# Turning the rotated queries and keys and the differential heads' outputs on VectorE and by block transfers, with score tiles of their own, in a two-layer encoder trunk

## The chip, the cores and the metric

The kernel runs on one core of a Trainium2 chip. The metric is the device time of one execution in microseconds (us), the median of several. One profiled execution is read instruction by instruction. The engines go by the names of the profile: PE (TensorE, matrix products), PEld (its weight loads), DVE (VectorE), ACT (ScalarE), POOL (GpSimd), SP (SyncE, which here only issues DMAs). A name with a q at its end (SPq) is the engine's instruction queue. Each engine works its queue off in order.

## The reference, cut to what matters

Two layers run over 256 tokens of width 2048, all in fp32. Layer 0 mixes with dilated window attention (8 heads) beside differential attention (4 heads); layer 1 mixes with grouped-query attention (8 query heads on 2 key heads, normalised and rotated) beside neighbourhood attention (8 heads). A gated convolutional FFN follows each mixer.

```python
# differential attention (layer 0): two softmax maps, then a norm over each head's 256 outputs
p = jax.nn.softmax(logits, axis=-1)
w = p[:, :, 0] - lam * p[:, :, 1]
o_b = jnp.einsum("bhqk,bkhd->bqhd", w, vf)
o_b = rmsnorm(o_b, subln) * (1.0 - lambda_init)
# grouped-query attention (layer 1)
q_c = apply_rope(rmsnorm(q_c, q_norm), cos, sin)
k_c = apply_rope(rmsnorm(k_c, k_norm), cos, sin)
o_c = gqa_block_attention(q_c, k_c, v_c)
# both layers
mixed = jnp.concatenate([out_1, out_2], axis=-1)
h = h + jnp.einsum("bse,ed->bsd", mixed, w_out)
h = h + conv_ffn(rmsnorm(h, ln_ffn), ...)
```

## The kernel before

**Products.** Each fp32 operand is split into a high part (rounded to fp32r, by ACT) and a rest (by DVE), and a product is three products of such parts: high by high, high by rest, rest by high. The helper is `split` (L239; `split_scaled`, L245, scales as well), so most casts and subtractions stand under L240 and L243.

**Weights** come in units of 512 KB, 128 partitions by 1024 numbers. `wunit` (L116) issues one DMA on SP (L125) into one of five `raw` tiles and splits it into one of four `wh` and four `wl` tiles. `gemm_a` (L208, products L204 to L206) makes a 256x512 chunk from eight or eleven units, twelve products each. `gemm_b` (L151, products L142 and L148) makes two 128x256 feature tiles from four units: high products of all units first, then the rests. Products accumulate in PSUM: four banks "gm" for the gemms, two "s" for scores and head outputs, two "tp" for what PE transposes.

**Order.** One clock of ticks lays the small work between the large. `tick` advances after every two units of `gemm_a` and twice in a `gemm_b`, so a tick is about two units. `later(d, f, rank)` (L91) puts off `f` by d ticks, `flush` (L103) ticks until nothing is pending. The functions only write instructions down in this order; the framework then sets the order of each engine's queue by its own reckoning of what is ready, keeping dependencies, so an instruction can stand ahead of one written earlier.

**Turning.** A 128x128 block is turned in one of two ways. `transpose_block` (L302) uses PE, by products with the identity (L305), into a "tp" bank. `turned` (L286) lets DVE transpose each 32x32 square in place (L288) and then `moved` (L278) carries the squares to their places by sixteen DMAs (L282), of which SP and POOL issue eight each, row by row in turn.

**Differential heads.** For each of the four heads, `gemm_b` makes q and k for both maps, `b_logits` and `b_softmax` follow two ticks later, `b_softmax` turns the weights (`turned`), three ticks later `b_transposes` splits them, one tick later `b_values` (L748) multiplies by the values: twelve products (L755 to L757), squares and a square root on ACT, and the scaled rows `o` (tile `ob`, L765). One tick later `b_finish` (L768) transposes `o` by PE, four blocks, and splits it into the head's two `mix` tiles, which the output projection reads. The values' order of tokens is by parity; `parity_rev` puts it straight.

**Output projection.** `mixer_out` (L369) makes four chunks of eight units; unit u reads `mix` tiles 2u and 2u+1. It runs units 0 to 6 of chunks 0 and 1 (four "gm" banks), then flushes, then runs unit 7 of both and chunks 2 and 3. Tiles 14 and 15, unit 7's, are the last head's.

**Grouped-query heads.** `norm_rope` (L838) normalises and rotates; its results are the row tiles `ry`. Three ticks later `to_features` (L872) transposes them by PE and splits them into the `cq` tiles: two key heads in one call, four query heads in each of two calls. The heads of a group follow at one a tick: `c_head` (L902) makes scores (`logits`, L426 to L428), takes the exponent on ACT (L910) into a tile `scc`, of which there are two for all heads, and `finish_head` (L888) turns it into a place in `room` (heads 0, 1, 4, 5) or in a pair tile (2, 3, 6, 7). Three ticks later the turned weights are split (tile `pt`), and a tick later `head_out` (L462, products L467 to L469) makes the head's output. The neighbourhood heads (`d_head`, L917) share `finish_head` and `scc`; one comes every two ticks.

Of the kernel before, what the change touches and what calls it, by code (L numbers as in the profile page):

```python
# [68 lines left out]
def trunk_kernel(ctx: ExitStack, tc, a, out):  # L69
# [155 lines left out]

    def parity(ap):

        return bass.AP(tensor=ap.tensor, offset=ap.offset, ap=[list(ap.ap[0]), [1, P], [P, 2]])
# [140 lines left out]
    def mixer_out(src, act, gain):  # L369
# [3 lines left out]
        for c in range(2):  # L373
            for u in range(7):
                a_unit(pss[c], src[c], u, act, KT)
                if u % 2 == 1:
                    tick()
        flush()
        for c in range(2):
            a_unit(pss[c], src[c], 7, act, KT)  # L380
            finish_chunk(pss[c], c, gain, res, 1 + c)
# [366 lines left out]
    def b_values(hd, pt, vt):  # L748
# [17 lines left out]
        later(1, lambda: b_finish(hd, o), 0)  # L766

    def b_finish(hd, o):  # L768
        ps = two(tps("tp", 2))
        transpose_block([(ps[:, f, t * P:(t + 1) * P], o[:, t, f * P:(f + 1) * P])  # L770
                         for f in range(2) for t in range(2)])
        for f in range(2):
            y = new_act("mix", 8 + 2 * hd + f)
            split_scaled(natural(y[:, 0, :]), natural(y[:, 1, :]), parity_rev(ps[:, f, :]), sub_gain[:, f:f + 1])
            mix[8 + 2 * hd + f] = y
# [96 lines left out]
    def to_features(ys, nh, slot):  # L872
        res = []
        ps = [two(tps("tp", 2)) for _ in range(nh // 2)]
        transpose_block([(ps[i // 2][:, i % 2, t * P:(t + 1) * P], ys[t][:, i, :])
                         for i in range(nh) for t in range(2)])
        for i in range(nh):
            q = new_qk("cq", slot + i)
            split(q[:, 0, :], q[:, 1, :], ps[i // 2][:, i % 2, :])
            res.append(q)  # L880
        return res
# [6 lines left out]
    def finish_head(sc, vt, cs, order, slot):  # L888
        if slot >= 8 or slot % 4 < 2:
            pf = room[:, slot % 2 * 4:slot % 2 * 4 + 4]  # L890
        else:
            if slot % 4 == 2:
                pairs[0] = pair_tile(22)
            pf = pairs[0][:, slot % 2 * 4:slot % 2 * 4 + 4]
# [5 lines left out]
        later(3, probs, 1)  # L900

    def c_head(q, k, vt, cs, slot):  # L902
# [5 lines left out]
        sc = tmp.tile([P, 2, SEQ], F32, name=nm("scc"), tag="scc")  # L908
# [26 lines left out]
    later(3, lambda ys=ys: kc.extend(to_features(ys, 2, 4)))  # L935
    for n in range(2):
# [3 lines left out]
        def c_heads(n=n, ys=ys):  # L940
            for i, q in enumerate(to_features(ys, 4, 0)):
                later(1 + i, lambda i=i, q=q: c_head(q, kc[n], cv, slice(n * P, (n + 1) * P), 4 * n + i))
        later(3, c_heads)
# [218 lines left out]
```

## Time and profile before

| | us |
|---|---|
| timed runs, median of 3 | 2466.28 (2465.97 to 2466.30) |
| the profiled execution, its own time | 2461.37 |
| its span, first to last instruction | 2459.6 |
| VectorE busy | 1636.1 |
| ScalarE busy | 1261.4 |
| products of the gemms' high parts, L142 | 956.8 |
| all transposes by PE of `ob` and `ry`, L305, 36 | 5.7 |

A row of a timeline gives start, duration, engine, line, operation, tiles written and read, and in brackets the idle time of the engine before it with what ended it. The durations of products overlap, since products are pipelined; the distance from start to start is what one costs. A row of the waits gives who waited for whom, the total, the number and the longest. A row of the windows gives the stretch, its length, and for PE, PEld, DVE, ACT and POOL the busy time with the number of instructions.

### The profile page before, as it was taken

To read this page: it belongs to the slowest core of one execution; us is meant where nothing else is said; L and a number is where in the kernel's file an instruction comes from. 1 tells how busy PE (TensorE), PEld (TensorE's weight loads), DVE (VectorE), ACT (ScalarE), POOL (GpSimd) and SP (SyncE) were. 2 spreads that over 40 slices of the span, in tenths; PEclk is the share of its full clock that TensorE was granted. 3 is DMA by queue.
4 is the path that set the end of the run, shared out by engine and by line. 5 is a ranking of instruction groups with operands and counts; after the bars stand their busy time and mean duration, and the time that the engine had idled before them with its cause. 6 is when DMAs were issued, how large, how long until landed. Compare 5 with 4: busy or idle time off the path is not lost.

```text
span 2459.6 us, 35236 instructions
## 1 busy us (share of the span) xinstructions
PE 2441.2 (99%) x12926; PEld 2108.2 (86%) x12926; DVE 1636.1 (67%) x2480; ACT 1261.4 (51%) x1876; POOL 198.3 (8%) x356
## 2 busy tenths in 40 slices
PE   9999999999999999999999999999999999999998
PEld 8888888888788888888888887888888888888887
DVE  6577577676676774477775568776767654676754
ACT  6555455565655443454544466555554533545443
POOL 1011012011200000000001106432000000000000
PEclk9999999999999999999999999999999999999999
DMA  8566566556655556565566655757555565555564
GB/s 310 184 200 191 172 195 210 174 181 198 199 184 194 186 198 196 180 198 183 195 197 207 209 175 152 224 176 224 192 184 196 181 206 196 180 192 186 193 201 146
DMA packets 194477, 476.12 MB, mean 194 GB/s; under 512 B 75384, under 2 KB 78200, under 8 KB 194304
## 3 DMA queue, kind: packets, MB, share of 16 engines
q1 hardware_dynamic: 182480, 461.09, 57.3%
q0 software_dynamic: 11392, 12.13, 2.8%
q8 instruction: 101, 1.65, 0.3%
q14 instruction: 72, 0.59, 0.1%
q10 hardware_dynamic: 432, 0.66, 0.1%
HBM read 458.48 MB, written 2.18 MB: 187 GB/s over the span
## 4 chain that ended last, share of the span: by engine, by line
PE 94%; DMA 2%; DVE 1%; ACT 1%; issue 1%; SPq 1%; POOL 0%; DVEq 0%; POOLq 0%; ACTq 0%
PE gm L142 36%; PE gm L148 19%; PE gm L205 12%; PE gm L204 12%; PE gm L206 12%; SPq L282 1%; DMA pair<-scc 0%; ACT wh L240 0%; DVE wl L243 0%; DMA room<-scc 0%; DMA hT<-z 0%; PE tp L305 0%; DMA raw<-in_od_out 0%; DMA raw<-in_od_qk 0%; PE s L428 0%
## 5 line engine op out<-in xcount | busy, mean ns | idle before, releaser
L243 DVE TENSOR_TENSOR wl<-raw,wh 128x1024 fp32r<-128x1024 f32 (+1 forms) x860 | 1034.5, 1216 | 563.0 <-ACT wh L240 328.1
L240 ACT CAST wh<-raw 128x1024 fp32r<-128x1024 f32 (+1 forms) x860 | 897.1, 1047 | 713.6 <-PE gm L206 375.8
L142 PE MATMUL gm<-yT,wh 128*128 128x512 f32 x4096 | 956.8, 390 | 3.5 <-ACT wh L240 3.0
L142 PEld LDWEIGHTS gm<-yT,wh 128*128 128x128 f32 x4096 | 760.3, 188 | 159.2 <-ACT wh L240 4.9
L148 PEld LDWEIGHTS gm<-yT,wl 128*128 128x128 f32 x4096 | 507.7, 192 | 9.3
L148 PE MATMUL gm<-yT,wl 128*128 128x256 f32 x4096 | 511.8, 283 | 0.0
L204 PE MATMUL gm<-wh,prod 128*128 128x512 f32 x702 | 273.2, 389 | 0.0
L205 PE MATMUL gm<-wl,prod 128*128 128x512 f32 x702 | 273.2, 389 | 0.0
L206 PE MATMUL gm<-wh,prod 128*128 128x512 f32 x702 | 273.1, 389 | 0.0
L233 ACT COPY t<-gm 128x256 f32<-128x256 f32 x256 | 95.2, 372 | 276.9 <-PE gm L148 276.9
L204 PE MATMUL gm<-wh,yT 128*128 128x512 f32 x412 | 161.6, 394 | 0.0
L205 PE MATMUL gm<-wl,yT 128*128 128x512 f32 x412 | 161.5, 392 | 0.0
L206 PE MATMUL gm<-wh,yT 128*128 128x512 f32 x412 | 161.3, 392 | 0.0
L204 PEld LDWEIGHTS gm<-wh,prod 128*128 128x128 f32 x702 | 131.8, 188 | 27.4
L206 PEld LDWEIGHTS gm<-wh,prod 128*128 128x128 f32 x702 | 131.8, 188 | 27.3
L205 PEld LDWEIGHTS gm<-wl,prod 128*128 128x128 f32 x702 | 131.8, 188 | 27.1
L234 DVE TENSOR_TENSOR t<-t,gm 128x256 f32<-128x256 f32 x256 | 105.5, 412 | 1.0 <-ACT t L233 0.8
L282 POOL DMA_DIRECT2D hT<-z x72 | 41.4, 583 | 785.0 <-ACT junk L274 681.0
L204 PE MATMUL gm<-wh,mix 128*128 128x512 f32 x256 | 99.9, 390 | 0.6 <-ACT mix L246 0.6
L205 PE MATMUL gm<-wl,mix 128*128 128x512 f32 x256 | 99.9, 390 | 0.4 <-DVE wl L243 0.4
L206 PE MATMUL gm<-wh,mix 128*128 128x512 f32 x256 | 99.3, 389 | 0.0
L206 PEld LDWEIGHTS gm<-wh,yT 128*128 128x128 f32 x412 | 77.8, 189 | 16.3
(247 smaller groups left out, 1669.3 us busy)
## 6 DMA issues: line engine op xcount, KB each, us to landing
raw<-in_up SPq DMA_DIRECT2D x352, 512.0 KB, 4.3
raw<-in_down SPq DMA_DIRECT2D x176, 512.0 KB, 4.2
raw<-in_eva_qk SPq DMA_DIRECT2D x96, 512.0 KB, 4.3
raw<-in_eva_v SPq DMA_DIRECT2D x46, 512.0 KB, 4.4
raw<-in_evb_qk SPq DMA_DIRECT2D x32, 512.0 KB, 4.2
raw<-in_ev_out SPq DMA_DIRECT2D x32, 512.0 KB, 4.3
raw<-in_od_qk SPq DMA_DIRECT2D x32, 512.0 KB, 4.8
raw<-in_od_out SPq DMA_DIRECT2D x32, 512.0 KB, 4.6
```

The source lines that it names most:

```text
L142: T.matmul(ps.rearrange("p a b -> p (a b)"), wh[:, k * P:(k + 1) * P], act[u * 8 + k].rearrange("p a b -> p (a b)"), start=(u == 0 and k = ...
L148: T.matmul(ps[:, 1, :], wl[:, k * P:(k + 1) * P], act[u * 8 + k][:, 0, :], start=False, stop=(last and u * 8 + k == KT - 1))
L204: T.matmul(ps[t], ah, wh[:, sl], start=(kt == 0), stop=False)
L205: T.matmul(ps[t], ah, wl[:, sl], start=False, stop=False)
L206: T.matmul(ps[t], al, wh[:, sl], start=False, stop=(kt == nk - 1))
L233: S.copy(t0, ps[:, 0, :])
L234: V.tensor_tensor(t0, t0, ps[:, 1, :], op=ALU.add)
L240: first = S.copy(dst_h, src)
L243: V.tensor_tensor(dst_l, src, dst_h.bitcast(F32), op=ALU.subtract)
L282: (nc.sync if i % 2 else G).dma_start(dst[j * 32:(j + 1) * 32, :, i * 32:(i + 1) * 32], z[i * 32:(i + 1) * 32].rearrange("p (b j c) -> p b ...
```

## The change

Five edits.

1. `b_values` turns `o` itself with `turned`, into a place among the activation tiles (slots 10, 12, 14, and 20 for the last head); `b_finish` comes three ticks later instead of one, transposes nothing and splits from that place. `halves_rev` reads it in the tokens' order.
2. `to_features` turns the rotated rows with `turned` (one call for each half of the tokens) two ticks after `norm_rope` instead of three, and hands back a function that splits them, which runs another two ticks later. So the heads of a group start one tick later.
3. Each grouped-query head has a score tile of its own (slots 8 to 15) and a place of its own for the turned scores (slots 0 to 7).
4. The turned weights of a grouped-query head are split four ticks after its scores instead of three.
5. `mixer_out` runs six units of chunks 0 and 1 before the flush instead of seven, and two behind it instead of one. Both layers use it.

```diff
+    def halves_rev(ap):
+        return bass.AP(tensor=ap.tensor, offset=ap.offset + 2 * SEQ - P - 1, ap=[list(ap.ap[0]), [-1, P], [-SEQ, 2]])
...
         for c in range(2):
-            for u in range(7):
+            for u in range(6):
                 a_unit(pss[c], src[c], u, act, KT)
                 if u % 2 == 1:
                     tick()
         flush()
         for c in range(2):
-            a_unit(pss[c], src[c], 7, act, KT)
+            for u in range(6, 8):
+                a_unit(pss[c], src[c], u, act, KT)
             finish_chunk(pss[c], c, gain, res, 1 + c)
...
-        later(1, lambda: b_finish(hd, o), 0)
-
-    def b_finish(hd, o):
-        ps = two(tps("tp", 2))
-        transpose_block([(ps[:, f, t * P:(t + 1) * P], o[:, t, f * P:(f + 1) * P])
-                         for f in range(2) for t in range(2)])
+        pf = (acts.tile([P, 4, P], F32, name=nm("oT"), tag=f"act{10 + 2 * hd}") if hd < 3
+              else pair_tile(20)[:, 0:4])
+        turned(o.rearrange("p t k -> p (t k)"), pf)
+        later(3, lambda: b_finish(hd, pf), 0)
+
+    def b_finish(hd, pf):
+        pv = pf.rearrange("p (t f) k -> p f t k", t=2)
         for f in range(2):
             y = new_act("mix", 8 + 2 * hd + f)
-            split_scaled(natural(y[:, 0, :]), natural(y[:, 1, :]), parity_rev(ps[:, f, :]), sub_gain[:, f:f + 1])
+            split_scaled(natural(y[:, 0, :]), natural(y[:, 1, :]), halves_rev(pv[:, f]), sub_gain[:, f:f + 1])
...
     def to_features(ys, nh, slot):
-        res = []
-        ps = [two(tps("tp", 2)) for _ in range(nh // 2)]
-        transpose_block([(ps[i // 2][:, i % 2, t * P:(t + 1) * P], ys[t][:, i, :])
-                         for i in range(nh) for t in range(2)])
-        for i in range(nh):
-            q = new_qk("cq", slot + i)
-            split(q[:, 0, :], q[:, 1, :], ps[i // 2][:, i % 2, :])
-            res.append(q)
-        return res
+        pf = pair_tile(20)
+        for t in range(2):
+            y = ys[t].rearrange("p n d -> p (n d)")[:, 0:nh * P]
+            turned(y, pf[:, t * 4:t * 4 + nh])
+
+        def tiles():
+            res = []
+            for i in range(nh):
+                q = new_qk("cq", slot + i)
+                split(*(q[:, x, :].rearrange("p (t k) -> p t k", t=2) for x in range(2)),
+                      pf.rearrange("p (t n) k -> p n t k", t=2)[:, i])
+                res.append(q)
+            return res
+        return tiles
...
     def finish_head(sc, vt, cs, order, slot):
-        if slot >= 8 or slot % 4 < 2:
+        if slot >= 8:
             pf = room[:, slot % 2 * 4:slot % 2 * 4 + 4]
         else:
-            if slot % 4 == 2:
-                pairs[0] = pair_tile(22)
-            pf = pairs[0][:, slot % 2 * 4:slot % 2 * 4 + 4]
+            pf = new_turned(f"act{slot}", pool=acts)
...
-        later(3, probs, 1)
+        later(3 if slot >= 8 else 4, probs, 1)
...
-        sc = tmp.tile([P, 2, SEQ], F32, name=nm("scc"), tag="scc")
+        sc = acts.tile([P, 2, SEQ], F32, name=nm("sch"), tag=f"act{8 + slot}")
...
-    later(3, lambda ys=ys: kc.extend(to_features(ys, 2, 4)))
+    def keys(ys=ys):
+        tiles = to_features(ys, 2, 4)
+        later(2, lambda: kc.extend(tiles()))
+    later(2, keys)
...
         def c_heads(n=n, ys=ys):
-            for i, q in enumerate(to_features(ys, 4, 0)):
-                later(1 + i, lambda i=i, q=q: c_head(q, kc[n], cv, slice(n * P, (n + 1) * P), 4 * n + i))
-        later(3, c_heads)
+            tiles = to_features(ys, 4, 0)
+
+            def heads():
+                for i, q in enumerate(tiles()):
+                    later(1 + i, lambda i=i, q=q: c_head(q, kc[n], cv, slice(n * P, (n + 1) * P), 4 * n + i))
+            later(2, heads)
+        later(2, c_heads)
```

## The prediction

> **What bounds the kernel now.** Part 1 of the page comes first, then the waits of PE, then PE's order of time around the places that the change touches.
>
> ```profile
> span 2459.6 us, 35236 instructions
> PE 2441.2 (99%) x12926; PEld 2108.2 (86%) x12926; DVE 1636.1 (67%) x2480; ACT 1261.4 (51%) x1876; POOL 198.3 (8%) x356
> ```
> ```profile
> PE gm L142 <- ACT wh L240: 3.0, 5, 1.4
> PE s L426 <- ACT scc L910: 2.7, 1, 2.7
> PE s L468 <- DVE pt L243: 1.4, 1, 1.4
> ```
>
> PE is idle for 18.4 us of the whole span; everything that is not PE work is a side stream that must not run late. A microsecond counts only if it leaves PE's queue or if PE waits for it. The waits quoted lie in the grouped-query stretch. So the change can win in two ways: fewer instructions on PE, and these waits. It can lose in one: by making PE wait for something that used to be in time.
>
> **The 36 transposes leave PE.** The tile view counts them, the order of time prices four of them.
>
> ```profile
> L305 PE MATMUL tp<-ident,ry x20: 270/272/328, 1436.7 to 1486.2; 128*128 128x128 f32 x20
> L305 PE MATMUL tp<-ident,ob x16: 270/272/328, 519.7 to 617.7; 128*128 128x128 f32 x16
> ```
> ```profile
> 519.45 0.39 PE L206 MATMUL gm<-wh,yT 128*128 128x512 f32 x1
> 519.68 0.60 PE L305 MATMUL tp<-ident,ob 128*128 128x128 f32 x4
> 520.03 0.48 PE L204 MATMUL gm<-wh,yT 128*128 128x512 f32 x1
> 520.35 0.40 PE L205 MATMUL gm<-wl,yT 128*128 128x512 f32 x1
> ```
>
> From start to start a 128x512 product takes 0.23 us here, the four transposes 0.35, and the product behind them 0.32: four transposes cost 0.35 + 0.09 = 0.44 us, not four times their 272 ns, which is latency. 36 are nine fours. The four of the last differential head belong to the next part; eight fours are **−3.5 us**. The splits that read the result keep their price (413 ns from PSUM, 412 from SBUF):
>
> ```profile
> L243 DVE TENSOR_TENSOR cq<-tp,cq 128x256 fp32r<-128x256 f32 x10 | 3.9, 413 | 0.5 <-ACT cq L240 0.4
> L243 DVE TENSOR_TENSOR qk<-t,qk 128x256 fp32r<-128x256 f32 x6 | 2.5, 412 | 0.0
> ```
>
> **What takes their place.** Ten calls of turned(): four for ob, four for the queries, two for the keys. Each is one 32x32 block transpose on VectorE, eight block DMAs on SP and eight on POOL. The first grouped-query head shows one:
>
> ```profile
> 1471.21 0.71 DVE L288 STREAM_TRANSPOSE scc<-scc 128x512 f32<-128x512 f32 x1 [0.19 <-ACT scc L913]
> ```
> ```profile
> 1471.95 5.11 SPq L282 DMA_DIRECT2D room<-scc  x8
> ```
> ```profile
> 1478.92 0.62 ACT L240 CAST pt<-room 128x512 fp32r<-128x512 f32 x1 [0.68 <-DMA room<-scc]
> ```
>
> SP issues for 5.11 us, and the reader, which waited for the landing, starts 7.0 us after the transpose ended (1471.92 to 1478.92). Where nobody waits this is free: 10 x 0.71 = 7 us at most on VectorE, which is 67% busy, 51 us of issuing on SP, and as many DMAs on POOL, which is 8% busy. It is not free at two places.
>
> **First place: the last differential head.** b_finish of head 3 runs in the flush() of mixer_out. Before:
>
> ```profile
> 613.44 0.28 PE L757 MATMUL s<-v,pt 128*128 128x256 f32 x1
> 613.56 0.40 PE L204 MATMUL gm<-wh,mix 128*128 128x512 f32 x1
> ...
> 616.08 0.39 PE L206 MATMUL gm<-wh,mix 128*128 128x512 f32 x1
> 617.03 0.94 PE L305 MATMUL tp<-ident,ob 128*128 128x128 f32 x4 [0.56 <-DVE ob L765]
> 618.54 0.50 PE L204 MATMUL gm<-wh,mix 128*128 128x512 f32 x1 [0.56 <-ACT mix L246]
> ```
> ```profile
> 616.49 0.88 DVE L765 TENSOR_SCALAR ob<-s,rb_h 128x256 f32<-128x256 f32 x2
> ```
> ```profile
> 618.01 0.47 ACT L246 ACTIVATE mix<-tp,sub_gain 128x256 fp32r<-128x256 f32 x1 [0.46 <-PE tp L305]
> ```
>
> b_values ends its issue at 613.56, one unit of the output projection (12 products, 2.7 us) covers to 616.31, and PE goes on at 618.54: 2.2 us lost. After the change the chain from 613.56 is 3.8 to the end of ob (617.37), 0.7 transpose, 7.0 blocks, 0.5 from the split's start to PE: 12.0 us. What covers it: units 6 of chunks 0 and 1, which the new loop bounds leave behind the flush, 2 x 2.7 = 5.4 us. Units 7 read this head's tiles, and chunks 2 and 3 need the four gm banks that chunks 0 and 1 hold. So PE stands still 6.6 us in place of 2.2: **+4.4 us**. Bounds: −2.2 if the chain shrank to its cover; +7.1 if PE's queue keeps chunk 0's unit 7 ahead of chunk 1's unit 6 and only 2.7 us covers. Behind the waiting split on ACT stand casts of chunk 2's weights, which PE can't use before units 7 are done. I take two units, since PE's queue is not bound to the program's order: here a product of the next gemm_b (L142) stands ahead of od_v's last unit.
>
> ```profile
> 1487.47 0.40 PE L142 MATMUL gm<-yT,wh 128*128 128x512 f32 x1
> 1487.71 0.40 PE L205 MATMUL gm<-wl,yT 128*128 128x512 f32 x1
> ```
>
> Such a stop costs more than itself. The windows view around the one long stop of before:
>
> ```profile
> 1490.00:1494.00 4.00, 1.29 (x6) 0.75 (x4) 0.62 (x1) 1.05 (x5) 2.97 (x6) 1.00 0.95 260
> 1494.00:1498.00 4.00, 3.98 (x11) 3.19 (x12) 3.68 (x7) 2.51 (x4) 1.87 (x4) 0.57 0.32 35
> ```
> ```profile
> 1490.45 0.84 PE L142 MATMUL gm<-yT,wh 128*128 128x512 f32 x3
> 1494.03 0.41 PE L426 MATMUL s<-cq,cq 128*128 128x256 f32 x1 [2.73 <-ACT scc L910]
> ...
> 1494.66 0.63 PE L206 MATMUL gm<-wh,yT 128*128 128x512 f32 x1
> 1495.09 0.63 PE L204 MATMUL gm<-wh,yT 128*128 128x512 f32 x1
> ```
>
> The last three figures are granted clock, DMA share and GB/s. The clock's mean is 0.57 after the stop, so 3.4 of the 4 us ran at half rate; products start 0.43 apart instead of 0.23, eight in that time: 1.6 us more. A 6.6 us stop at 617 will pay it too: **+1.6 us**. [...]
>
> The other three heads' blocks fall where SP stood waiting for a score transpose anyway: 0, at most +1.
>
> **Second place: the grouped-query stretch.** The 2.7 us wait ends on ACT's exp of the fourth head, whose score tile shares a buffer with the second's; a tile of its own takes that wait away. From 1491.1 (the product's turn) to 1494.03 are 2.9 us, with the slow clock 1.6 more: **−4.5 us**. What is late next? SP. It issues weight loads and blocks in one order:
>
> ```profile
> 1482.96 5.11 SPq L282 DMA_DIRECT2D room<-scc  x8
> 1488.17 0.53 SPq L125 DMA_DIRECT2D raw<-in_od_qk  x1
> 1488.91 12.60 SPq L282 DMA_DIRECT2D pair<-scc  x16
> 1501.55 1.06 SPq L125 DMA_DIRECT2D raw<-in_od_qk  x2
> 1504.94 5.19 SPq L282 DMA_DIRECT2D room<-scc  x8
> ```
>
> For 13 us no weights were asked for. The price came later:
>
> ```profile
> 1517.10 2.11 PE L142 MATMUL gm<-yT,wh 128*128 128x512 f32 x8 [1.41 <-ACT wh L240]
> ```
>
> A tick with a head asks SP for 5.1 + 1.1 = 6.2 us and PE for two units and twelve small products, 5.4 + 1.4 = 6.9. The change puts the second group's two query blocks into the ticks of heads 1 to 3 and shifts all heads one tick later, so that head 7 meets the first neighbourhood head. In those eight ticks SP has eleven blocks and sixteen loads, 56 + 9 = 65 us, against PE's 55: 10 short. The buffers (five raw, four cast) run up to nine units ahead; less the one in use, 4.8 us from issue to landing and 2.3 for the two casts, SP may lag 8 x 2.7 − 7.1 = 14.5 us (an estimate from those rows) before PE starves.
>
> ```profile
> raw<-in_od_qk SPq DMA_DIRECT2D x32, 512.0 KB, 4.8
> ```
>
> 10 is below 14.5, but not if the blocks stand together. The splits of the second group's queries wait on ACT for these blocks, and behind them the casts of wh; PE then lives on the cast units in hand, three of them, 8 us. The waits of PE there today, 3.0 + 1.4 = 4.4 us, I leave as they are: **0**, bounds −4.4 (all go) and +10 (the whole shortfall).
>
> In the neighbourhood part the new bounds of mixer_out only move the last head's values one unit forward; its blocks landed well before. 0.
>
> **Sum.** −3.5 + 4.4 + 1.6 − 4.5 + 0 = −2.0 us on the profiled execution (span 2459.6, its own time 2461.37). The timed runs' median, 2466.28, lies 4.9 above that second figure; I carry the difference over: **2464.3 us**. A measurement can tell 0.2% from no change, here 4.9 us, so this forecast counts as the same.
>
> **Rivals.**
> 1. *The stretch clears.* With own score tiles ACT never blocks, SP never stands still between blocks, and the 4.4 us go as well: −6.4, 2459.9; with the tail covered a little better, 2457. For it: the 13 us hole in the loads began behind blocks that waited for that same ACT. Against: SP gets six blocks more. Chance 0.27, faster.
> 2. *A convoy on SP.* Two query blocks and a head's block stand in a row behind a VectorE transpose that is still to come: over 15.4 us without a load. It decides from 14.5 us on; the group's logits then wait as well. Price 6 to 10 us with a slow clock behind it: 2470 to 2474. For it: the hole of 13 us exists today with two blocks. Against: PE's heads also move later. Chance 0.22, slower.
> 3. *One unit of cover at the tail*: +2.7, 2466.5, the same. Chance 0.1.
> 4. *The turn itself is the wrong engine's work*, a loss in every head, since each turn takes 7.7 us of latency against 0.44 on PE: if the readers came due before the blocks landed, the two query groups would add up to 2 x (7.7 − 0.4) = 15 us, less the tick of delay that they were given (one, 5.4 each): about +4, 2470. [...] The first head's row shows the latency, and that a delay of ticks hides it. Chance 0.06, counted with the slower ones only in half.
>
> The forecast itself has 0.35. Faster by over 0.2%: 0.27; slower: 0.22 + 0.03 = 0.25; the same 0.48. The range reaches into both neighbours: 2457.0 (rival 1) to 2473.0 (rival 2, less its worst).
>
> **What would show it.** No transposes of ry and ob on PE; a stop of 6 to 7 us before unit 7 of ev_out with a window of half clock behind it, and two units between b_values and the stop (one: rival 3); no wait of L426 for L910; on SP, blocks of the second query group between heads' blocks. Holes over 14 us there with waits of L142 behind them mean rival 2; no such waits, rival 1. If the blocks at the tail land much sooner than 7 us after their transpose, the first place is mis-sized.

## The result and the profile after

The changed kernel takes **2487.2 us** (median of four runs, 2486.3 to 2490.3) against 2466.1 us of the kernel before in the same comparison: ratio 1.0092, 95% interval 1.0080 to 1.0104. That is slower by some 21 us, where 2464.3 us was predicted, with a range up to 2473.0. The profiled execution of the changed kernel took 2486.4 us.

In the changed kernel's line numbers the logits are L431 to L433 (L426 to L428 before), the splits L244 and L247 (L240 and L243), the scaled splits L250 and L253 (L246 and L249), the block DMAs L286 (L282) and VectorE's transpose L292 (L288). The head of its page, and what PE waited for (total, times, longest):

```profile
span 2484.5 us, 35459 instructions
PE 2442.8 (98%) x12890; PEld 2109.0 (85%) x12890; DVE 1644.3 (66%) x2490; ACT 1260.8 (51%) x1874; POOL 241.9 (10%) x436
```
```profile
PE s L431 <- ACT cq L244: 8.0, 1, 8.0
PE gm L204 <- ACT mix L250: 7.9, 1, 7.9
PE s L431 <- ACT qk L244: 4.4, 2, 2.6
PE s L431 <- DVE mix L247: 3.8, 3, 1.5
```

The 36 matmuls are gone from PE (12890 for 12926), and so is the wait for a score tile. In their place stand two stops of 8 us, one at each of the two places of the prediction, and a row of smaller ones (the waits for weight casts, L142, are 3.2 us, before 3.0). By the order of time PE starts the odd mixer (its first transpose of h) at 1409.2 us instead of 1402.9, which is 6.3 us, and loses another 19 between there and the first product of od_out (1656.4 instead of 1630.7). Of those 19 us 17 are stops: over this stretch the windows view has PE busy for 222.7 of 247.1 us, before for 220.3 of 227.8. The two profiled executions lie 25 us apart and the medians 21, since that of before was 4.9 under its median.

**The first place.** PE, VectorE and ScalarE around the last differential head, in the order of time (start, duration, instruction, idle time before it and who ended it):

```profile
609.58 0.40 PE L204 MATMUL gm<-wh,mix 128*128 128x512 f32 x1
...
614.82 0.39 PE L206 MATMUL gm<-wh,mix 128*128 128x512 f32 x1
623.06 0.80 PE L204 MATMUL gm<-wh,mix 128*128 128x512 f32 x1 [7.86 <-ACT mix L250]
623.66 0.63 PE L205 MATMUL gm<-wl,mix 128*128 128x512 f32 x1
```
```profile
612.51 0.88 DVE L770 TENSOR_SCALAR ob<-s,rb_h 128x256 f32<-128x256 f32 x2
613.62 1.23 DVE L247 TENSOR_TENSOR wl<-raw,wh 128x1024 fp32r<-128x1024 f32 x1 [0.23 <-ACT wh L244]
614.76 0.71 DVE L292 STREAM_TRANSPOSE ob<-ob 128x512 f32<-128x512 f32 x1
```
```profile
622.45 1.02 ACT L250 ACTIVATE mix<-pair,sub_gain 128x256 fp32r<-128x256 f32 x2 [6.16 <-DMA pair<-ob]
```

From 609.58 to the last start at 614.82 PE runs 24 products without a pause: both units 6 cover, as predicted (rival 3, one unit, is out). The output tile is ready at 613.39, but a weight tile's low half stands ahead of its transpose on VectorE, which therefore ends at 615.47 and not at 614.1. Seven microseconds later ScalarE splits. PE stands 8.0 us beyond its usual 0.23 from start to start, and then starts nine products about 0.43 apart (the first 0.60).

**The second place.** SP in the grouped-query stretch, neighbours of one kind put together (SPq is SP's queue; the duration is that of issuing):

```profile
1480.16 2.44 SPq L125 DMA_DIRECT2D raw<-in_od_qk  x2
1489.16 5.11 SPq L286 DMA_DIRECT2D pf<-sch  x8
1494.64 3.16 SPq L286 DMA_DIRECT2D pair<-ry  x5
1497.91 5.11 SPq L286 DMA_DIRECT2D pf<-sch  x8
1503.07 7.96 SPq L286 DMA_DIRECT2D pair<-ry  x11
1511.15 10.35 SPq L286 DMA_DIRECT2D pf<-sch  x16
1521.55 0.59 SPq L125 DMA_DIRECT2D raw<-in_od_qk  x1
```

Six blocks, four of heads and two of the second query group, stand in a row: 48 DMAs and no weight load for 39 us. The first 6.6 of these SP does nothing at all: it stands before the first head's block until that head's transpose on VectorE has ended, and the loads stand behind.

```profile
1488.40 0.70 DVE L292 STREAM_TRANSPOSE sch<-sch 128x512 f32<-128x512 f32 x1
```

SP's record of this wait, and the block's first issue (number, shortest, median and longest in ns, first and last start in us):

```profile
L286 SPq EVENT_SEMAPHORE  x1: 6492/6492/6492, 1482.6 to 1482.6; - x1
L286 SPq DMA_DIRECT2D pf<-sch x1: 597/597/597, 1489.2 to 1489.2; - x1
```

The wait stands in SP's queue for 6.49 us, from 1482.6 to 1489.1. The transpose ended at 1489.10, the issue came at 1489.16, and the trace has no other DMA of SP between 1482.60 and there.

ScalarE hands this on, because its queue holds weight casts, splits and exps in one order:

```profile
1498.20 1.04 ACT L244 CAST wh<-raw 128x1024 fp32r<-128x1024 f32 x1
...
1513.12 1.33 ACT L244 CAST cq<-pair 128x256 fp32r<-128x256 f32 x4 [5.47 <-DMA pf<-sch]
...
1525.40 1.05 ACT L244 CAST wh<-raw 128x1024 fp32r<-128x1024 f32 x1
```

No weights are cast for 27 us. The releaser named for the split of cq is a head's block, but cq reads the query blocks, whose last DMA on SP began its issue before 1511.03 (the end of the row of eleven) and landed some 2 us later (median 2.1 for these blocks): it is the second group's tile that PE's logits wait 8.0 us for. Yet this tile in time would not have let PE go on for long: the first weights behind the hole are asked for at 1521.55 and cast at 1525.40, the first product that uses them starts at 1526.50, and from 1505.55 to there PE has nothing but the heads' small products. The windows view of the stretch in both kernels (PE, PEld, DVE, ACT and POOL busy, granted clock, DMA share, GB/s), the kernel before from 1484 on, the changed one from 1490 on:

```profile
1484.00:1499.00 15.00, 12.27 (x59) 9.94 (x58) 9.77 (x21) 8.10 (x21) 11.35 (x22) 0.89 0.53 112
1499.00:1514.00 15.00, 15.00 (x94) 13.52 (x93) 12.11 (x22) 8.63 (x21) 8.02 (x16) 1.00 0.63 144
1514.00:1529.00 15.00, 13.23 (x83) 11.40 (x82) 12.12 (x24) 9.14 (x22) 10.65 (x19) 1.00 0.60 166
```
```profile
1490.00:1505.00 15.00, 13.07 (x66) 11.16 (x67) 12.06 (x22) 6.80 (x18) 13.23 (x26) 1.00 0.32 51
1505.00:1520.00 15.00, 5.56 (x26) 5.07 (x25) 6.55 (x16) 5.80 (x16) 13.47 (x25) 0.59 0.35 58
1520.00:1535.00 15.00, 9.45 (x59) 7.86 (x57) 11.71 (x26) 8.04 (x23) 13.18 (x24) 0.96 0.49 105
```

Moved bytes fall to 51 and 58 GB/s, PE to 5.6 of 15 us, and the clock to 0.59. In these 45 us PE is busy 28.1 us, before 40.5.

### The profile page after: what moved, and what is told of

The parts are those of the page before. It is cut to its first block, busy times and chain, and to the rows that moved or that the text cites. A ratio compares the mean times of both kernels' runs of the same rounds, so it can differ in the third digit from the quotient of the medians.

```text
span 2484.5 us, 35459 instructions
## 1 busy us (share of the span) xinstructions
PE 2442.8 (98%) x12890; PEld 2109.0 (85%) x12890; DVE 1644.3 (66%) x2490; ACT 1260.8 (51%) x1874; POOL 241.9 (10%) x436
## 4 chain that ended last, share of the span: by engine, by line
PE 95%; SPq 2%; DMA 1%; POOL 1%; DVE 1%; issue 0%; ACT 0%; DVEq 0%; ACTq 0%
PE gm L142 36%; PE gm L148 19%; PE gm L204 12%; PE gm L205 12%; PE gm L206 12%; SPq L286 2%; DMA raw<-in_od_qk 1%; POOL pair L286 0%; PE s L431 0%; POOL pf L286 0%; PE s L433 0%; DMA room<-scc 0%; PE s L432 0%; PE s L666 0%; PE s L627 0%
## 5 line engine op out<-in xcount | busy, mean ns | idle before, releaser
L247 DVE TENSOR_TENSOR wl<-raw,wh 128x1024 fp32r<-128x1024 f32 (+1 forms) x860 | 1035.4, 1217 | 575.7 <-ACT wh L244 336.3
L244 ACT CAST wh<-raw 128x1024 fp32r<-128x1024 f32 (+1 forms) x860 | 897.2, 1047 | 709.8 <-PE gm L206 386.0
L142 PE MATMUL gm<-yT,wh 128*128 128x512 f32 x4096 | 957.1, 391 | 3.2 <-ACT wh L244 3.2
L142 PEld LDWEIGHTS gm<-yT,wh 128*128 128x128 f32 x4096 | 761.6, 188 | 158.5 <-ACT wh L244 4.2
L286 POOL DMA_DIRECT2D hT<-z x72 | 41.4, 583 | 767.3 <-ACT junk L278 719.3
L205 PEld LDWEIGHTS gm<-wl,yT 128*128 128x128 f32 x412 | 77.4, 188 | 18.2 <-DVE wl L247 2.7
```

The source lines that it names most:

```text
L142: T.matmul(ps.rearrange("p a b -> p (a b)"), wh[:, k * P:(k + 1) * P], act[u * 8 + k].rearrange("p a b -> p (a b)"), start=(u == 0 and k = ...
L205: T.matmul(ps[t], ah, wl[:, sl], start=False, stop=False)
L244: first = S.copy(dst_h, src)
L247: V.tensor_tensor(dst_l, src, dst_h.bitcast(F32), op=ALU.subtract)
L286: (nc.sync if i % 2 else G).dma_start(dst[j * 32:(j + 1) * 32, :, i * 32:(i + 1) * 32], z[i * 32:(i + 1) * 32].rearrange("p (b j c) -> p b ...
```

## The experiments

Each kernel was timed against the kernel before on the same chip; the ratio's 95% interval stands beside it. The ratio on record isn't the quotient of the two medians (2487.2 by 2466.1 is 1.0086), so a difference of medians is good to some 2 or 3 us. "Hole" is the longest time between the starts of two weight loads on SP in the grouped-query stretch, with the number of SP's block DMAs in it; "odd mixer" is the time from its first transpose of h to the first product of od_out. Both are from the one profiled execution of each kernel. The changed kernel, e1 and e15 run the odd mixer's instructions in the same order on every engine and take 247.1, 248.6 and 249.8 us, so a difference below 3 us in that column says little.

| kernel | median us | ratio to before | hole us (DMAs) | odd mixer us |
|---|---|---|---|---|
| before | 2465.1 to 2466.1 | 1 | 13.4 (16) | 227.8 |
| changed | 2487.2 | 1.0092 (1.0080 to 1.0104) | 39.3 (48) | 247.1 |
| e9 outputs alone, on before | 2471.6 | 1.0029 (1.0018 to 1.0041) | 12.8 (16) | 226.6 |
| e4 score tiles alone, on before | 2467.3 | 1.0010 (1.0001 to 1.0019) | 14.4 (16) | 233.1 |
| e5 16 dead DMAs on SP, on before | 2476.6 | 1.0043 (1.0031 to 1.0055) | 35.0 (48) | 240.5 |
| e12 8 dead DMAs on SP, on before | 2466.4 | 1.0007 (0.9998 to 1.0015) | 24.2 (32) | 231.2 |
| e11 16 dead DMAs on POOL, on before | 2461.6 | 0.9988 (0.9980 to 0.9997) | 10.4 (8) | 227.5 |
| e8 six of 16 blocks on SP, on before | 2478.4 | 1.0053 (1.0041 to 1.0065) | 12.8 (6) | 237.3 |
| e13 second group's heads apart, on before | 2465.0 | 1.0004 (0.9995 to 1.0013) | 12.6 (16) | 230.2 |
| e10 outputs of heads 0 to 2, on before | 2461.3 | 0.9985 (0.9976 to 0.9994) | 13.0 (8) | 231.5 |
| e6 second group by PE, on changed | 2477.6 | 1.0043 (1.0030 to 1.0057) | 12.1 (8) | 232.8 |
| e2 queries and keys by PE, on changed | 2478.2 | 1.0049 (1.0035 to 1.0063) | 14.6 (16) | 235.3 |
| e3 shared score tiles, on changed | 2489.9 | 1.0101 (1.0087 to 1.0115) | 39.1 (48) | 249.6 |
| e1 outputs by PE, on changed | 2485.6 | 1.0083 (1.0069 to 1.0097) | 39.2 (48) | 248.6 |
| e15 the same, odd loop kept | 2485.4 | 1.0084 (1.0070 to 1.0098) | 39.0 (48) | 249.8 |
| e7 six of 16 blocks on SP, on changed | 2496.2 | 1.0122 (1.0109 to 1.0135) | 31.1 (36) | 247.0 |
| e16 second group on POOL, on changed | 2482.8 | 1.0074 (1.0061 to 1.0086) | 28.3 (40) | 242.3 |
| e17 e16 and last output by PE | 2474.0 | 1.0037 (1.0024 to 1.0049) | 29.8 (40) | 241.8 |

### Which part costs what: one part undone or alone

e1 gives b_values, b_finish and mixer_out the text of before; e2 gives it to to_features and its callers (with their delay of three ticks); e4 puts the changed finish_head and score tile into the kernel before, and e3 is e4's reverse on the changed kernel. The cores of e1, e2 and e4:

```diff
-        turned(o.rearrange("p t k -> p (t k)"), pf)
-        later(3, lambda: b_finish(hd, pf), 0)
+        later(1, lambda: b_finish(hd, o), 0)
...
-            for u in range(6):
+            for u in range(7):
```
```diff
-            turned(y, pf[:, t * 4:t * 4 + nh])
+        transpose_block([(ps[i // 2][:, i % 2, t * P:(t + 1) * P], ys[t][:, i, :])
+                         for i in range(nh) for t in range(2)])
```
```diff
-        sc = tmp.tile([P, 2, SEQ], F32, name=nm("scc"), tag="scc")
+        sc = acts.tile([P, 2, SEQ], F32, name=nm("sch"), tag=f"act{8 + slot}")
...
-        if slot >= 8 or slot % 4 < 2:
+        if slot >= 8:
...
-        later(3, probs, 1)
+        later(3 if slot >= 8 else 4, probs, 1)
```

> The changed kernel, with the differential heads' outputs turned by TensorE again and seven units ahead of the flush in mixer_out; the queries, the keys and the score tiles stay as changed. In the traces the changed kernel reaches the odd mixer 6.3 us later than the kernel before. Theory tail (8.0 us stop plus half clock at the end of layer 0, less 1.3 us for the other three heads): all 6.3 come back, 2481 us, and the stretch of the grouped queries keeps its 18 us of loss. Rival (the stretch only starts in a bad place because layer 0 ends late): the stretch changes as well and the time moves by over 10 us, either way.

> The changed kernel, with the rotated queries and keys turned by TensorE again, at the delays of before; score tiles in places of their own and the outputs by blocks stay. Theory T1 (the query and key blocks in SP's one queue hold the weight loads back): the 18.6 us of the stretch go, and the wait for a shared score tile stays gone (4.5 to 9 us better than before there), so before + 6.3 - 4.5 to 9: 2463 to 2468 us, and no hole over 14 us in SP's weight loads. Rival T2 (score tiles of their own let the heads' blocks bunch up by themselves): 2480 us or more, with long holes still there.

> The changed kernel, with the grouped heads' score tiles in the two shared buffers again and their blocks in the places and with the delay of before; queries and keys and the differential outputs stay by blocks. T1 (query and key blocks in SP's queue): still slow, 2478 to 2492 us, with a hole of over 25 us in the weight loads. T2 (the score tiles in places of their own are the harm): 2470 to 2473 us, the tail's 6.3 us being all that is left of the loss.

> The kernel before, with nothing but the grouped heads' score tiles and their turned tiles in places of their own, and the delay of four ticks instead of three behind the blocks. T1: the wait for the shared tile goes (2.9 us and 1.6 us of half clock) and perhaps the other waits of the stretch: 2457 to 2462 us, faster than before. T2: bunched blocks make it 2470 us or more. If it is 2464 to 2468, the place of the score tiles matters neither way and the wait was only moved.

e2 took 9 us off, not the 19 or more expected: the queries' and keys' blocks are a large part of the loss, not all of it. e3 stayed slow, with the hole still there, so the score tiles are not the main harm. But e4 refutes the gain that the prediction had booked for them, and that T1 took over from it: alone they cost 1.9 us (e4's median less 2465.4 of before; the interval of the ratio just excludes 1). PE's largest wait in e4 and what ScalarE did meanwhile:

```profile
PE s L426 <- ACT sch L908: 5.7, 1, 5.7
```
```profile
1501.22 0.62 ACT L240 CAST pt<-pf 128x512 fp32r<-128x512 f32 x1 [0.23 <-DMA pf<-sch]
1507.51 1.04 ACT L240 CAST wh<-raw 128x1024 fp32r<-128x1024 f32 x1 [5.67 <-DMA raw<-in_od_qk]
1509.57 1.04 ACT L240 CAST wh<-raw 128x1024 fp32r<-128x1024 f32 x1 [1.02 <-DMA raw<-in_od_qk]
1510.53 0.47 ACT L908 ACTIVATE sch<-s,mx 128x256 f32<-128x256 f32 x1
```

The exp no longer waits for a buffer. It stands behind two casts that wait for weights, and those were asked for late because SP had two heads' blocks to issue first. The wait of L426 is there again, 5.7 us for 2.7, with another name at its root.

e1 misses: undoing the outputs gave back 1.6 us of 6.3. The first place is taken up by itself further down.

### Is it SP's time, or the latency of the tiles?

e5 adds to the kernel before, at the second query group, a copy of its rotated queries into a tile that nobody reads; the queries themselves go through PE as before. No engine that computes gets more work.

```diff
         def c_heads(n=n, ys=ys):
+            if n:
+                dead = pair_tile(20)
+                for t in range(2):
+                    z = ys[t].rearrange("p n d -> p (n d)")
+                    for i in (1, 3):
+                        for j in range(4):
+                            nc.sync.dma_start(
+                                dead[j * 32:(j + 1) * 32, t * 4:t * 4 + 4, i * 32:(i + 1) * 32],
+                                z[i * 32:(i + 1) * 32].rearrange("p (b j c) -> p b j c", j=4, c=32)[:, :, j, :])
```

e12 copies with `i in (1,)`, half as much; e11 with `i in (0, 2)` and `G.dma_start`, on POOL. e6 is the changed kernel with to_features of before, under the name by_pe, for the second group alone:

```diff
-            tiles = to_features(ys, 4, 0)
+            tiles = (lambda: by_pe(ys, 4, 0)) if n else to_features(ys, 4, 0)
```

> The kernel before, with 16 more DMAs on SP at the second query group: it copies that group's rotated queries, not transposed, block by block into a tile that nobody reads, and the queries themselves still go through TensorE. Nothing waits for the copies, so only SP's time is added (16 x 0.64 = 10 us). Theory T1, now as 'SP's issuing is what bounds the grouped-query stretch': the weight loads behind them come up to 10 us late, waits of the weight casts on PE grow, 2471 to 2477 us. Rival T3 (what costs is the latency of the second group's tiles, which PE's logits wait for): no change, 2463 to 2468 us.

> The kernel before, with 8 dead block copies on SP in place of 16 (5.1 us of SP instead of 10.3). Without any slack on SP, as 11.5 us for 10.3 suggests: +5 to 6, 2470 to 2472 us. With the lead of several loads that the prediction counted on (14.5 us): no change, 2464 to 2468 us, and the cost of 16 would come from a step behind that lead.

> The kernel before, with 16 dead block copies of the second query group as in the run with dead blocks on SP (+11.5 us), but issued by POOL, which issues no weight loads. If SP's time is what costs: 2464 to 2468 us, no change. If any queue that carries half of each turn will do (POOL's half of the heads' blocks late, ACT's casts waiting for them): 2470 us or more.

> The changed kernel, with the second query group alone turned by TensorE (keys and first group stay on blocks). In the first four runs the score tiles alone cost 4.7 us in this stretch of the trace, and the blocks of queries and keys some 14 more. T1 (SP's time): the six blocks in a row become four, no 8 us wait of the logits for cq, the stretch loses 5 to 10 us against before instead of 18.6, total 2474 to 2480 us. Rival: if the keys' and the first group's blocks, with one tick more of delay for all heads, are the cause, it stays at 2484 us or more.

Sixteen dead DMAs on SP cost 11.5 us (2476.6 less 2465.1), and nothing reads their tile. Sixteen on POOL cost nothing. Taking the second group's sixteen out of the changed kernel gives 9.6 us back (2487.2 less 2477.6), and the 8.0 us wait of L431 for cq is gone. So the price is SP's queue, and the latency of the tiles isn't needed for it. By the traces e6 makes the odd mixer 14 us shorter (247.1 to 232.8) and the output projection behind it 5 us longer (from its first product to its last 95.9 for 90.6), which wasn't explained. SP in e5:

```profile
1478.27 1.00 SPq L125 DMA_DIRECT2D raw<-in_od_qk  x2
1481.55 3.83 SPq L947 DMA_DIRECT2D pair<-ry  x6
1485.47 6.32 SPq L282 DMA_DIRECT2D room<-scc  x8
...
1508.74 5.09 SPq L282 DMA_DIRECT2D room<-scc  x8
1513.88 0.59 SPq L125 DMA_DIRECT2D raw<-in_od_qk  x1
```

The same kind of hole as in the changed kernel, 35 us, and nothing in it that PE had not needed before; ScalarE casts no weights for 26.5 us (1491.3 to 1517.8). The copies are not all of this hole. The framework built SP's queue in another order as well: three weight loads that stand between the blocks of the second to fifth head in the kernel before stand behind the fifth head's in e5. And in e11 a load stands between the third and the fourth head's blocks, where before has none (hole 10.4 for 13.4). What the added issues cost and what the order costs can't be told apart here; both are SP's queue. It also means that e11's 3.5 us of gain may be its order's, and may hide a small price of POOL's copies. Half the copies make a hole of 24 us and cost 1.4 us, which can't be told from none: the loads do have a lead, and it had run out at 35. The keys' and first group's blocks cost nothing that shows (e2 against e6).

### The other side: giving POOL more

moved() lets POOL issue ten of a turn's 16 blocks and SP six, for the heads (e8) and for heads, queries and keys (e7); e16 lets POOL issue all 32 of the second group.

```diff
-                (nc.sync if i % 2 else G).dma_start(
+                (nc.sync if i % 2 and j < sp else G).dma_start(
```

with sp = 3 in e7 and e8, and 0 for the second group (4 elsewhere) in e16.

> The changed kernel, with SP issuing 6 and POOL 10 of the 16 blocks of each turn in the odd mixer (8 and 8 as changed): SP's block falls from 5.1 to 3.9 us, POOL's grows from 4.35 to 5.5 us. T1 (SP's time bounds the stretch): the eleven blocks of the eight ticks take 13 us less of SP, so 6 to 12 us come back, 2475 to 2481 us. Rival T3 (the latency of a turned tile decides): POOL's half ends 1.1 us later, so no gain or a small loss, 2486 to 2491 us.

> The kernel before, with SP issuing 6 and POOL 10 of the 16 blocks of each head's turn in the odd mixer. T1: if SP's time bounds the stretch already in the kernel before, its weight loads come up to 1.3 us a head earlier, the casts' waits on PE (4.4 us) and part of the 2.9 us wait go: 2458 to 2463 us. If SP was not yet the bound there: 2464 to 2468 us.

> The changed kernel, with all 32 block DMAs of the second query group issued by POOL (16 by SP and 16 by POOL as changed); everything else as changed. If the second group costs by the 10 us that it takes of SP: 2475 to 2480 us, as without its blocks at all, though its own tiles come some 9 us later. If it costs by its latency: 2487 us or more.

e7 and e8 lie outside both of their forecasts, 9 and 13 us slower than the kernels that they are built on, though SP has less to issue. The DMA part of the page points to the reason (the last figure is the median from issue to landing), first of before, then of e8:

```profile
room<-scc SPq DMA_DIRECT2D x96, 16.0 KB, 2.1
room<-scc POOLq DMA_DIRECT2D x96, 16.0 KB, 1.8
```
```profile
room<-scc POOLq DMA_DIRECT2D x120, 16.0 KB, 3.1
room<-scc SPq DMA_DIRECT2D x72, 16.0 KB, 2.6
```

Issued ten to a turn, POOL's blocks land 3.1 us after their issue, not 1.8, and SP's get later as well (2.6 for 2.1). The casts of pt wait for them on ScalarE, ahead of the casts of weights. One such place in e8, ScalarE and then PE:

```profile
1649.54 0.62 ACT L240 CAST pt<-room 128x512 fp32r<-128x512 f32 x1 [6.15 <-DMA room<-scc]
```
```profile
1653.15 0.50 PE L205 MATMUL gm<-wl,mix 128*128 128x512 f32 x1 [3.66 <-DVE wl L243]
```

So a late tile does cost here too, by the same queue of ScalarE; it is a second way in, not the one that the changed kernel took. The waits of pt for the room tiles add up to 35.5 us on ScalarE in e8, before to 27.6. That this makes up all of the 13 us isn't shown. And the loss lies in good part behind the grouped-query stretch: in e8's trace the odd mixer takes 9.5 us more than before and the output projection behind it 11.8 more (102.3 for 90.5); in e7 the odd mixer takes as long as in the changed kernel, and the projection 7 us longer (97.8 for 90.6). The 8 us shorter hole of e7 gained nothing.

e16 lies between its two forecasts, 4.4 us better than the changed kernel. The second group's queries are split 11 us later there against the mixer's start (1525.05 for 1513.12), and PE nowhere waits for them. It waits for weights:

```profile
PE gm L142 <- ACT wh L244: 18.3, 3, 9.9
```

The heads' own blocks still stand together. Twenty-four DMAs of three heads make a hole of 21 us here, and ScalarE feels it at once:

```profile
1520.87 1.04 ACT L244 CAST wh<-raw 128x1024 fp32r<-128x1024 f32 x1 [10.20 <-DMA raw<-in_od_qk]
```

Another hole of 12 us ended just before, with two loads between them. So the lead is no fixed time: 21 us behind another 12 had used it up here, where 24 us cost 1.4 in e12. That it is what the loads before have put by is an estimate from these two.

e13 spaces the second group's heads in the kernel before, one to two ticks:

```diff
-            q = new_qk("cq", slot + i)
+            q = (acts.tile([P, 2, SEQ], F32R, name=nm("cq"), tag=f"act{12 + i}") if apart
+                 else new_qk("cq", slot + i))
...
-                later(1 + i, lambda i=i, q=q: c_head(q, kc[n], cv, slice(n * P, (n + 1) * P), 4 * n + i))
+                later(1 + n + (1 + n) * i, lambda i=i, q=q: c_head(q, kc[n], cv, slice(n * P, (n + 1) * P), 4 * n + i))
```

> The kernel before, with the second group's four heads one to every two ticks instead of one to every tick, their query tiles in places that are free until the last neighbourhood heads. Nothing is added or taken away on any engine. If SP's time in those ticks is what PE waits for (6.2 of 6.9 us a tick, with the waits for VectorE on top): the 4.4 us for weight casts and part of the 2.9 us for a score tile go, 2458 to 2463 us. If the spacing makes the later heads meet the neighbourhood heads' blocks instead: 2464 us or more.

No change, and hardly a shorter hole: 12.6 us where before has 13.4. The spacing did not reach what it was meant for.

### The first place by itself

Here mixer_out takes the number of units ahead of the flush as an argument, one for each layer:

```diff
-    def mixer_out(src, act, gain):
+    def mixer_out(src, act, gain, n):
...
-            for u in range(7):
+            for u in range(n):
```

e9 is the kernel before with b_values and b_finish as changed, six units in layer 0 and seven in the odd mixer. e15 is the changed kernel with b_values and b_finish of before, seven units in layer 0 and six in the odd mixer. e10 is e9 with the last head by PE:

```diff
+        if hd == 3:
+            later(1, lambda: b_finish_pe(hd, o), 0)
+            return
+        pf = acts.tile([P, 4, P], F32, name=nm("oT"), tag=f"act{10 + 2 * hd}")
         turned(o.rearrange("p t k -> p (t k)"), pf)
```

with b_finish_pe as b_finish was before. e17 is e16 with this edit.

> The kernel before, with the differential heads' outputs by block transfers and six units ahead of the flush in layer 0 alone (the odd mixer keeps seven). Theory tail: 8.0 us of stop and 1.6 of half clock in place of 2.2 us, less 1.3 for twelve transposes: +6.3, 2470 to 2473 us. Rival (what the first run suggested, which gave only 1.6 back when the outputs were undone): the odd mixer's order swallows it and it stays within 2464 to 2468 us.

> The changed kernel with the differential outputs by TensorE and seven units in layer 0, as in the first run, but with the odd mixer's loop left at six units as changed. The outputs alone cost 6.5 us on the kernel before. If they add up with the rest and the first run lost it by its seven units in the odd mixer: 2479 to 2482 us. If the odd mixer eats the gain whatever its loop: 2484 us or more.

> The kernel before, with the outputs of differential heads 0 to 2 by block transfers, the last head's still by TensorE, and six units ahead of the flush in layer 0, so that two units and not one cover the last head's chain. Theory tail: 1.3 us of transposes leave PE and the 2.2 us stop is covered: -3.5, 2460 to 2463 us. Rival (the outputs' blocks cost in any place): 2465 us or more.

> The changed kernel, with both losses mended: the second query group's blocks on POOL and the last differential head's output by TensorE. If the two add up (about -9 and -8 to -10): 2467 to 2473 us, level with the kernel before or a little above; the score tiles' 2 us stay. If one of them was only hidden by the other, 2476 us or more.

e9 costs 6.5 us (2471.6 less 2465.1), and its trace has the stop of the changed kernel to the tenth:

```profile
PE gm L204 <- ACT mix L250: 7.9, 1, 7.9
```

In e10 the stop is gone, that of before too: the transposes run at once, among products.

```profile
613.54 0.48 PE L205 MATMUL gm<-wl,mix 128*128 128x512 f32 x1
613.86 0.49 PE L309 MATMUL tp<-ident,ob 128*128 128x128 f32 x3
```

With e11, e10 is the fastest of all, 2461.3 us, below both kernels (0.9985, 0.9976 to 0.9994) and inside its forecast. That its gain of 4 us is the 3.5 predicted can't be claimed from the time alone: e11, which only adds dead copies, came out 3.5 us ahead of before as well, and in the traces e10's output projection of layer 0 takes 92.5 us from its first product to its last, only 0.9 less than before. e17 against e16 gives 8.8 us for the last head's output; its 2474.0 us lie 1 us above the forecast, since e16 brought 4.4 us and not 9.

e15 misses like e1. Its instructions in the odd mixer stand in the same order on every engine as in the changed kernel, yet it takes 2.7 us longer there and 3 more in od_out, which eats the 6.3. Its stops in the odd mixer are no longer. The windows view from the mixer's first transpose to the first product of od_out, changed kernel first, then e15:

```profile
1409.23:1656.35 247.12, 222.68 (x1147) 189.68 (x1146) 170.50 (x309) 134.22 (x269) 103.03 (x184) 0.97 0.58 173
```
```profile
1403.34:1653.18 249.84, 227.78 (x1147) 194.07 (x1146) 170.54 (x309) 134.28 (x269) 102.79 (x184) 0.94 0.58 171
```

The same 1147 products keep PE busy 5.1 us longer at a lower mean clock, and PE is idle 22.1 us against 24.4. So what eats the gain there is half clock: behind the hole it lasts 20.5 us in e15 and 13.7 in the changed kernel (why it lasts longer in e15 wasn't shown). Of the 3 us in od_out 1.7 are stops of PE; the rest is open.

One smaller loss can be seen as well. One of SP's issues for the first query group takes 2.34 us where its fifteen neighbours take 0.6. The split of cq comes 2.2 us later against the mixer's start, and PE, which had no wait there in the changed kernel, stops:

```profile
1472.05 0.39 PE L431 MATMUL s<-cq,cq 128*128 128x256 f32 x1 [2.11 <-ACT cq L244]
```

## Why the prediction was wrong, step by step

- **The transposes, −3.5.** PE has 36 matmuls less. In layer 0 the first product of ev_out comes at 573.3 instead of 574.1, with two of the fours ahead of it: 0.4 each. Single executions scatter by 1 us here; over the nine kernels that turn these outputs by blocks (573.0 to 574.2) and the nine that use PE (574.1 to 575.1) the means differ by 1.0, 0.5 each. Right there; the five fours of queries and keys weren't priced by themselves.
- **The last differential head, +4.4 and +1.6.** The mechanism was right: two units of cover, seven microseconds of turn, half clock behind. It was mis-sized. The stop was 8.0 us and not 6.6, since a low half of weights got ahead of the transpose on VectorE (1.1 us and its gaps), and the slow products cost 1.9 (nine, 0.2 more each), not 1.6. The sum with the three other heads was +4.7; the traces show +6.3, and e9, timed alone, +6.5.
- **The score tile's wait, −4.5.** This step failed. The wait of L426 for the shared tile did go, but e4 is 1.9 us slower, not 4.5 faster. The prediction asked what is late next, named SP, and priced it at 0 (with bounds of −4.4 and +10). In e4 the same logits wait 5.7 us through ScalarE's casts for loads that SP issued late.
- **The other waits of the stretch, 0.** This is the step that failed by most. The prediction compared demand with supply over eight ticks (65 us of SP against 55 of PE, 10 short) and set that against a lead of 14.5 us, as if the blocks were spread, though it said itself that this doesn't hold if they stand together. They were not spread: the first group's heads came later and met the second group's blocks, six blocks in a row, with SP idle for 6.6 us at their head. That is rival 2, whose chance was put at 0.22; its hole was to be over 15.4 us and was 39. Its price of 6 to 10 us fits the second group's blocks alone (9.6 by e6; e5's copies, with the loads put behind them, cost 11.5). Its time of 2470 to 2474 us was too low, because it was reckoned on top of a gain from the score tiles that wasn't there and a tail that was too cheap. The sign that it named, waits of L142 behind the hole, is not what the changed kernel shows (3.2 us, before 3.0): there the logits stand ahead of those products and take the wait. The lead of 14.5 us was no fixed figure: a hole of 24 us cost 1.4 us in e12, one of 21 behind another of 12 left ScalarE idle for 10 in e16.
- **The sum.** e9's 6.5, e4's 1.9 and e6's 9.6 make 18.0 of the 21 us. The 3 left are of the size of the comparisons' intervals; e1 and e15 show besides that the parts don't simply add. In the prediction's own arithmetic rival 3 is off: 2.7 on top of 2464.3 is 2467.0, not 2466.5; nothing rests on it.
- **Rival 4**, latency as such, wasn't what happened to the changed kernel, whose logits waited for a tile that SP issued late; in e16 the tile came later still and nothing waited for it. e7 and e8 are where late tiles do cost: on the kernel before, 1.3 us more landing time on POOL's part of every turn came with 13 us more.
- **Rival 1**, that the stretch clears once ScalarE waits for no score tile, fell with e4.

## What to carry to other kernels

Where weight loads and other DMAs share one issuing queue, look for the longest stretch without a load in the built order, with the waits of whatever heads that queue, and not for the mean demand: here 24 us without one cost nothing that shows, and 35 and 39 went with losses of some ten. A wait that goes away on an engine with one queue can uncover the next entry of that queue (in e4 the logits' 2.7 us for the score tile became 5.7 behind two casts of weights); price that entry before booking the gain. A DMA added to a queue can also move the loads of that queue in the built order (three of them in e5); read the order before putting a price on the DMA. Turn a tile by DMA only where work that doesn't need it lasts longer than the whole turn (here 13.5 us from the last value product to PE, against 5.4 of cover).

## What the runs showed of the hardware

The same block DMA takes SP 0.60 us to issue, but now and then 0.9 to 2.3 us: ten times in the trace of the kernel before (0.90 to 2.05 us), eight times in that of the changed kernel (0.98 to 1.70). e15's 2.34 us fall among the sixteen issues for the first query group, where the changed kernel, with the same SP program in the odd mixer, has no such issue (eight in 5.13 us and eight in 5.10). The cause is open. In a stretch without slack this one stopped PE for 2.1 us (e15).

The clock after a stop did not fall at a fixed time. In the changed kernel PE's last product before the stop at 615 ended at 615.2:

```profile
618.00:622.00 4.00, 0.00 (x0) 0.00 (x0) 0.00 (x0) 0.00 (x0) 2.36 (x5) 0.77 0.34 55
...
626.00:630.00 4.00, 4.00 (x16) 3.22 (x16) 2.71 (x4) 2.40 (x5) 0.00 (x0) 0.88 0.00 0
```

A mean of 0.77 is 1.8 of 4 us at half rate, so the clock fell at about 620.2, 5.0 us after the last product; a mean of 0.88 puts its return at 627.0, 6.8 us later. In the kernel before the last product ended at 1491.3, PE went on at 1494.03, and the clock fell only then:

```profile
1494.00:1495.00 1.00, 0.97 (x3) 0.88 (x4) 0.68 (x3) 1.00 (x3) 0.55 (x1) 0.62 0.80 67
```

A mean of 0.62 is 0.76 of 1 us, so it fell at 1494.24, 2.95 us after the last product, and the 0.57 that the prediction shows for 1494 to 1498 makes it 3.4 us long. The changed kernel has two more such stretches in its odd mixer. The clock's means over 1507 to 1508, 1521 to 1522, 1538 to 1539 and 1541 to 1542 are 0.81, 0.86, 0.67 and 0.62, which by the same reckoning puts one at 1507.6 to 1521.3, 13.7 us, and one at 1538.3 to 1541.8, 3.4 us. With the 20.5 us of e15 these lengths, 3.4, 6.8, 13.7 and 20.5, are 3.41 us and whole multiples of it. What sets when the clock falls and when it returns wasn't shown. The fifth 3.4 us of e15's stretch hold 2.50 us of PE's work and the half clock goes on; the last 3.4 us of the changed kernel's 13.7 hold 2.93:

```profile
1518.79:1522.21 3.42, 2.50 (x12) 2.21 (x11) 2.60 (x7) 2.57 (x6) 3.40 (x6) 0.50 0.66 188
```
```profile
1517.87:1521.28 3.41, 2.93 (x12) 2.64 (x12) 1.88 (x6) 2.03 (x8) 0.60 (x2) 0.50 0.35 62
```

So the price of a stop was not one figure here: behind the 2.7 us of before the half clock lasted 3.4 us, behind the changed kernel's 7.9 it lasted 6.8, of which PE was at work for 3.9. The 1.6 us that the prediction booked for half clock is the price of the first of these.
